# Staging slots, a shorter w2 ring, swapped pools and a re-ordered last norm in a float32 trunk layer

## The chip, the cores and the metric

One core of a Trainium2 chip. The metric is the device time of one execution in microseconds (us); the time before is the median of three executions. The engines are TensorE (PE), VectorE (DVE), ScalarE (ACT), GpSimd (POOL) and SyncE (SP, which here issues DMAs only). All instructions of one engine run in the order of the program.

## What is computed

One layer of a trunk on 2048 positions of width 1024, all in float32: a token mixer (left as it is here) and a feed-forward part.

```python
def reference(x, ...):
    h = x
    for l in range(DEPTH):                     # DEPTH = 1
        y = rmsnorm(h, pre_mix_g[l])
        ...
        h = h + rmsnorm(m, post_mix_g[l])
        f = rmsnorm(h, pre_ff_g[l]) @ w_ff1[l]           # 2048x1024 @ 1024x4096
        f = jnp.square(jax.nn.relu(f)) @ w_ff2[l]        # 2048x4096 @ 4096x1024
        h = h + rmsnorm(f, post_ff_g[l])
    return h
```

## The kernel before

**Stages.** In the trace the mixer runs to about 783 us, the first product of the feed-forward part (FF1) from there to about 1430, the second (FF2) from 1431 to the end. A float32 product is made of three matmuls in a split form: each operand is a high part (a cast by ACT) and a low part (a difference by VectorE); `mm3` (L142) does low x high, high x high, high x low, and `split_lo` (L139) makes the low part. Both products of the feed-forward part use one level of Winograd's scheme, so that a block product takes seven (p1 to p7) and not eight, on operands that are sums of quarters.

**FF1.** `seq` lists 224 ticks: 32 steps (two passes p over halves of the positions, 16 steps q over w1), each with seven products; a tick is one product, 12 matmuls of 128x512. Work of the other engines is planned to ticks by hand: `plan(tick, fn, ...)` appends to a tick's list and `do(tick)` runs the list after the tick's matmuls and its evacuation. The right operand `ht` (the transposed h, 28 tiles, each high and low) belongs to a pass and is replaced at the change of pass, ticks 104 to 114. `ht_in(1, n)` reads tile n into a staging slot (hr) on SP, and `ht_split` splits it; the slots are the four of the tag `four`. Two pools lie next to each other here: `fr` with the ring `w2s` (three tiles of 128x1024) and `wq` with the split w1 tiles `wh` and `wl`.

**W2 in FF1's shadow.** W2 is cut into 16 quarters q; `read_w2` reads one into `w2s`, `sum_w2` makes the sums t1 to t4 on VectorE, and `split_w2` casts (ACT), subtracts (VectorE) and stores both parts (th and tl) to memory, `t_d`, by the queue of POOL. The parts lie in the same four `four` slots. `when(j)` gives the tick of a quarter's j-th job: the ticks from 36 on, 11 a quarter, with the ticks of the change of pass left out (`away`).

**End of FF1.** The result of a step lies in ux and uy (128x1024 each) and is written to `f_d` on SP, a tick after its last operation (`keep_f`).

**FF2.** 16 chunks m = (p, c): two passes p, eight slices c of the inner dimension. A chunk has seven products in the order p1, p6, p5, p7, p4, p3, p2, each for four row tiles r: 28 slots of 6 matmuls. The right operand tt (1 MB a product, three buffers, read on SP two products ahead) comes from `t_d`. The left operand of the next chunk is made from f (512 KB reads on SP) by the jobs of `PREP`, planned to slots by `plan2`: a sum is VectorE's, a split is a cast on ACT (sh) and a difference on VectorE (sl). `SHIFT` delays the jobs of some chunks. After a slot's matmuls `evac` takes its bank: in a pass's first chunk ACT copies it into an accumulator (`acc`, 28 tiles), later VectorE adds it. In the last chunk of a pass the rows are finished: ACT sums squares (jq), `root` makes 1/rms with VectorE and a POOL power, `scale` multiplies by it and by post_ff_g, `give` adds the residual (hr) and writes the row to `out`. Rows of a pass come in two sets of four, from p7 and p4 (rows 4 to 7, later 12 to 15) and from p3 and p2 (rows 0 to 3, later 8 to 11).

**Order around the end of a pass.** In a slot the planned jobs come first, then the list `soon` (roots of the slot before), then `evac`. After pass 0 a list `tail` holds 16 jobs, one taken per slot of chunk 8: for each row a `scale`, and `pair_up` with the other `scale`, two residual additions on POOL and two writes by POOL's queue. After pass 1 POOL multiplies each half by post_ff_g (`weigh`, 12 times), and VectorE finishes with one operation a half (`finish_row`).

## Time and profile before

| | us |
|---|---|
| median of three executions | 2112.43 (2110.93 to 2113.45) |
| the profiled execution | 2111.22 |
| its span in the trace | 2109.5 |
| PE busy | 2020.6 (96%) |
| DVE busy | 1428.3 (68%) |
| ACT busy | 996.9 (47%) |
| POOL busy | 279.6 (13%) |

The profile is of one execution, and its span is 1.7 us shorter than that execution's time. Shares of the whole span are averages over the stages; TensorE's two clock levels are 2.4 GHz (granted clock 1.00) and 1.2 GHz (0.50). Rows of the trace stand below, in groups, where the prediction reads them.

### The profile page before, as it was taken

What the parts mean: (1) busy time and instruction counts of PE and PEld (TensorE: products, weight loads), DVE (VectorE), ACT (ScalarE), POOL (GpSimd) and SP (SyncE); (2) the same over time, 40 slices, a digit from 0 to 9 for tenths busy, and PEclk for the clock granted to TensorE, in tenths of its full rate; (3) what the DMA queues carried; (4) which work ended last, traced back from release to release, by engine and by line L of the source; (5) the groups of instructions that cost most, each with busy time, mean ns of one, the idle gap of its engine ahead of it and who ended that gap; (6) DMA issues with size and microseconds to landing.
All of it is one profiled execution on the core that took longest, in us unless ns stands there. A gap on an engine that the chain in (4) does not pass through costs nothing.

```text
span 2109.5 us, 27460 instructions
## 1 busy us (share of the span) xinstructions
PE 2020.6 (96%) x9504; PEld 1660.1 (79%) x9504; DVE 1428.3 (68%) x2463; ACT 996.9 (47%) x1966; POOL 279.6 (13%) x427
## 2 busy tenths in 40 slices
PE   8999999999899998999998999998999998999994
PEld 6888878888788877888876888886888886788883
DVE  3484467357646776666667666665788888988884
ACT  5463465356345556566667666666222225322112
POOL 0020011002101100022211222220000004200004
PEclk9999999999999999999999999999999999999997
DMA  6444244425843457768777877778667666776655
GB/s 211 123 116 131 80 135 144 157 76 176 251 154 98 158 189 219 254 250 273 258 254 256 281 260 250 269 265 316 236 229 269 239 223 241 284 268 241 259 188 191
DMA packets 164716, 446.86 MB, mean 212 GB/s; under 512 B 23376, under 2 KB 48480, under 8 KB 150240
## 3 DMA queue, kind: packets, MB, share of 16 engines
q1 hardware_dynamic: 139040, 359.09, 50.8%
q0 software_dynamic: 25536, 86.00, 11.2%
q8 instruction: 75, 1.23, 0.2%
q14 instruction: 65, 0.53, 0.1%
HBM read 319.19 MB, written 125.83 MB: 211 GB/s over the span
## 4 chain that ended last, share of the span: by engine, by line
PE 76%; DVE 8%; DMA 7%; ACT 4%; issue 3%; POOL 2%; SPq 0%; POOLq 0%; ACTq 0%; DVEq 0%
PE pf_A L143 5%; PE pf_A L144 5%; PE pf_A L145 5%; PE po_A L144 5%; PE po_A L143 5%; PE po_A L145 5%; PE pp_o L143 3%; PE pp_o L145 2%; PE pp_o L144 2%; PE pf_C L143 2%; PE pf_C L145 2%; PE pf_C L144 2%; PE po_C L144 2%; PE po_C L143 2%; PE po_C L145 2%
## 5 line engine op out<-in xcount | busy, mean ns | idle before, releaser
L493 DVE TENSOR_TENSOR acc_p<-acc_p,po_A 128x512 f32<-128x512 f32 x224 | 153.6, 686 | 21.8 <-PE po_A L145 6.7
L953 ACT CAST sh_s<-r 128x512 fp32r<-128x512 f32 x96 | 56.7, 619 | 186.0 <-PE po_A L145 118.7
L140 DVE TENSOR_TENSOR wl_s<-s,wh_s 128x512 fp32r<-128x512 f32 x96 | 66.2, 689 | 71.9 <-ACT wh_s L691 71.8
L143 PE MATMUL pf_A<-hl_t,wh_s 128*128 128x512 f32 x256 | 102.3, 400 | 12.6 <-ACT uy L878 9.1
L143 PE MATMUL po_A<-tt,sh_a 128*128 128x512 f32 x256 | 102.0, 398 | 8.3 <-DMA tt<-t_d_b 6.0
L143 PE MATMUL po_A<-tt,sh_s 128*128 128x512 f32 x256 | 100.8, 394 | 6.9 <-DVE acc_p L493 3.1
L143 PE MATMUL pp_o<-wl_o,abh 128*128 128x512 f32 x256 | 103.3, 404 | 2.1 <-DVE h L450 1.9
L953 ACT CAST sh_a<-f 128x512 fp32r<-128x512 f32 x96 | 57.5, 620 | 99.5 <-PE po_C L144 37.7
L144 PE MATMUL po_A<-tt,sh_a 128*128 128x512 f32 x256 | 102.1, 399 | 0.0
L145 PE MATMUL po_A<-tt,sl_a 128*128 128x512 f32 x256 | 101.8, 398 | 0.0
L144 PE MATMUL pf_A<-hh_t,wh_s 128*128 128x512 f32 x256 | 101.7, 397 | 0.0
L145 PE MATMUL pf_A<-hh_t,wl_s 128*128 128x512 f32 x256 | 101.4, 396 | 0.0
L144 PE MATMUL po_A<-tt,sh_s 128*128 128x512 f32 x256 | 101.2, 395 | 0.0
L145 PE MATMUL po_A<-tt,sl_s 128*128 128x512 f32 x256 | 100.9, 394 | 0.0
L218 DVE SCALAR_TENSOR_TENSOR wl_o<-ws_o,outg,wh_o 128x512 fp32r<-128x512 f32 x64 | 47.9, 749 | 78.0 <-ACT wh_o L217 78.0
L144 PE MATMUL po_C<-tt,sh_s 128*128 128x512 f32 x256 | 100.5, 393 | 0.0
L145 PE MATMUL pp_o<-wh_o,abl 128*128 128x512 f32 x256 | 100.4, 392 | 0.0
L144 PE MATMUL pp_o<-wh_o,abh 128*128 128x512 f32 x256 | 100.3, 392 | 0.0
L143 PE MATMUL po_C<-tt,sh_s 128*128 128x512 f32 x256 | 99.9, 390 | 0.4 <-DMA tt<-t_d_t 0.4
L145 PE MATMUL po_C<-tt,sl_s 128*128 128x512 f32 x256 | 100.2, 391 | 0.0
L140 DVE TENSOR_TENSOR wl_a<-w1s,wh_a 128x512 fp32r<-128x512 f32 x96 | 65.9, 687 | 45.3 <-ACT wh_a L691 45.2
L217 ACT ACTIVATE wh_o<-ws_o,outg 128x512 fp32r<-128x512 f32 x64 | 46.3, 723 | 100.7 <-PE pp_o L145 56.2
(292 smaller groups left out, 6069.0 us busy)
## 6 DMA issues: line engine op xcount, KB each, us to landing
tt<-t_d_t SPq DMA_DIRECT2D x64, 1024.0 KB, 4.8
tt<-t_d_b SPq DMA_DIRECT2D x48, 1024.0 KB, 4.8
w1s<-in_w SPq DMA_DIRECT2D x64, 512.0 KB, 4.9
f<-f_d SPq DMA_DIRECT2D x64, 512.0 KB, 7.1
ws_o<-in_w_out SPq DMA_DIRECT2D x64, 256.0 KB, 2.5
w2s<-in_w POOLq DMA_DIRECT2D x32, 512.0 KB, 5.7
t_d_t<-th_t POOLq DMA_DIRECT2D x64, 256.0 KB, 4.7
t_d_t<-tl_t POOLq DMA_DIRECT2D x64, 256.0 KB, 4.7
```

Of the source, the lines that this page charges most:

```text
L140: v.tensor_tensor(out_lo, src, hi.bitcast(F32), ALU.subtract)
L143: pe.matmul(ps, ahi, blo, start=start, stop=False, **kw)
L144: pe.matmul(ps, ahi, bhi, start=False, stop=False, **kw)
L145: pe.matmul(ps, alo, bhi, start=False, stop=stop, **kw)
L217: a.activation(hi, st, AF.Copy, scale=gain)
L218: v.scalar_tensor_tensor(lo, st, gain, hi.bitcast(F32), ALU.mult, ALU.subtract)
L493: eng.tensor_tensor(out_, x_, y_, ALU.add)
L953: a.copy(hi, src)
```

## The change

1. **Staging at FF1's change of pass.** The 28 reads of the second pass use 12 slots and not four: the four `four` slots, two `hts` slots and six halves of the `w2s` ring. Their reads are planned further ahead, and the splits stand at the front of their tick's list.
2. **w2 ring.** A quarter takes 10 ticks and not 11, from tick 44 and not 36.
3. **Pools.** `ga` (accumulators) and `gt` (tt) change places on the right side, so that tt lies over `fr`, and the accumulators over `wq`. The first chunk's a11 splits lie in the ring `h` of another pool.
4. **Splits of the left operand** become two jobs: `high_f` (ACT's cast) before `evac` and `low_f` (VectorE's difference) after it. Roots come after `evac`, a slot after their last square. `SHIFT` covers one chunk more.
5. **End of pass 0.** `tail` holds four jobs a row (32), one a slot and two in each fourth; the residual additions are VectorE's, the writes stay on POOL's queue.
6. **End of pass 1.** `weigh` and `finish_row` are gone; a row's root comes a slot after its last square and its scalings and additions two slots after. The additions of rows 12 to 15 are POOL's, those of rows 8 to 11 VectorE's, the writes go by SP.

```diff
     def ht_in(p, n):
-        staged[p, n] = slot(f"hr{p}_{n}", tag="four") if p else stage(f"hr{p}_{n}")
-        read_ht(p, n, staged[p, n])
+        if p == 0:
+            st = stage(f"hr{p}_{n}")
+        elif n % 12 < 4:
+            st = slot(f"hr{p}_{n}", tag="four")
+        elif n % 12 < 6:
+            st = wp.tile([P, 512], F32, name=f"hr{p}_{n}", tag="hts", bufs=2)
+        else:
+            if n % 2 == 0:
+                staged["two"] = fr.tile([P, D], F32, name=f"hr{p}_{n}", tag="w2s", bufs=3)
+            st = staged["two"][:, n % 2 * H:(n % 2 + 1) * H]
+        staged[p, n] = st
+        read_ht(p, n, st)
...
     for n in range(28):
-        plan(at[NQ - 1, FIRST[n // 4]] + 1, ht_in, 1, n)
-        plan(at[NQ - 1, FIRST[n // 4]] + 2, ht_split, 1, n)
+
+        plan(at[NQ - 1, FIRST[n // 4 - 3]] + 2 if n >= 12 else at[NQ - 1, "p1"] + 1 + n // 8, ht_in, 1, n)
+    for n in range(28):
+        todo.setdefault(at[NQ - 1, FIRST[n // 4]] + 2, []).insert(n % 4, (ht_split, (1, n)))
...
-    free = [t for t in range(36, len(seq)) if t not in away]
+    free = [t for t in range(44, len(seq)) if t not in away]
     for q in range(NQ):
         def when(j):
-            return free[11 * q + j]
+            return free[10 * q + j]
...
-            (5, sum_w2, "t3"), (6, split_w2, "t1"), (7, split_w2, "t3"), (8, sum_w2, "t4"), (9, split_w2, "t4"),
-            (10, split_w2, "b22"),
+            (4, split_w2, "t2"), (5, split_w2, "t1"), (6, sum_w2, "t4"), (7, split_w2, "t3"), (8, split_w2, "t4"),
+            (9, split_w2, "b22"),
...
+    ga = ctx.enter_context(tc.tile_pool(name="ga", bufs=1, side="right", reuse_waits="tile"))
     gt = ctx.enter_context(tc.tile_pool(name="gt", bufs=1, side="right", reuse_waits="tile"))
-    ga = ctx.enter_context(tc.tile_pool(name="ga", bufs=1, side="right", reuse_waits="tile"))
...
-    SHIFT = {NC: 12, NC + 1: 9, NC + 2: 6, NC + 3: 3}
+    SHIFT = {NC: 12, NC + 1: 12, NC + 2: 9, NC + 3: 6, NC + 4: 3}
...
-    def give(i, hf, eng):
+    def give(i, hf, eng, queue):
         plus(eng, res[i][hf], res[i][hf], halves[i, hf])
-        queue = pool if eng is pool else dma
         queue.dma_start(out[i * P:(i + 1) * P, hf * 512:(hf + 1) * 512], res[i][hf])
...
+        if hf:
+            return
+        soon.setdefault(slot_ + 1, []).append((root, row_))
         if p < NP - 1:
-            if done:
-                tail.extend(((scale, row_, 0), (pair_up, row_)))
-            return
-        if n != "p2":
-            weigh(row_, hf)
-        if n == "p4":
-            soon.extend(((finish_row, row_, 0), (finish_row, row_, 1)))
-        elif n == "p2":
-            soon.extend(((finish_row, row_, 1), (scale, row_, 0), (give, row_, 0, v)))
+            tail.extend(((scale, row_, 1), (give, row_, 1, v, pool), (scale, row_, 0), (give, row_, 0, v, pool)))
+        else:
+            eng = pool if row_ == j else v
+            soon.setdefault(slot_ + 2, []).extend((
+                (scale, row_, 1), (give, row_, 1, eng, dma), (scale, row_, 0), (give, row_, 0, eng, dma)))
...
+                for fn, args in todo2.pop((slot_, 0), ()):
+                    fn(*args)
+                evac(m, n, r, banks[chain, r])
                 for fn, args in todo2.pop(slot_, ()):
                     fn(*args)
-                for fn, *args in soon:
+                for fn, *args in soon.pop(slot_, ()):
                     fn(*args)
-                soon.clear()
-                evac(m, n, r, banks[chain, r])
-                if tail and c < NC - 1:
...
+                for _ in range((2 if slot_ % 4 == 3 else 1) if c < NC - 1 else 0):
+                    if tail:
+                        fn, *args = tail.pop(0)
+                        fn(*args)
+
+                        nth = 8 - len(tail) // 4
+                        if len(tail) % 4 == 0 and 2 <= nth < 6:
+                            read_h(nth - 2)
```

**SP at FF1's change of pass**, from the fourth read of the new right operand (hr1_3) on; w1s are halves of w1 for a coming step, f_d writes are results of step 14. Before:

```order
L526 DMA hr1_3_10911<-ht_d2_95 128x512
L668 DMA w1s17_0_10930<-in_w1 128x1024
L850 DMA f_d0_14_111<-ux14_10699 128x1024
L850 DMA f_d0_14_111<-uy14_10700 128x1024
L526 DMA hr1_4_10991<-ht_d2_95 128x512
L526 DMA hr1_5_10993<-ht_d2_95 128x512
L526 DMA hr1_6_10995<-ht_d2_95 128x512
L526 DMA hr1_7_10997<-ht_d2_95 128x512
L668 DMA w1s17_1_11018<-in_w1 128x1024
L524 DMA hr1_8_11036<-b_d1_0_133 128x512
L524 DMA hr1_9_11038<-b_d1_1_134 128x512
L524 DMA hr1_10_11040<-b_d1_2_135 128x512
```

After, from the same place in the queue:

```order
L526 DMA hr1_3_10899<-ht_d2_95 128x512
L526 DMA hr1_4_10901<-ht_d2_95 128x512
L526 DMA hr1_5_10903<-ht_d2_95 128x512
L526 DMA hr1_6_10905<-ht_d2_95 128x512 x2
L668 DMA w1s17_0_10941<-in_w1 128x1024
L524 DMA hr1_8_10943<-b_d1_0_133 128x512
L524 DMA hr1_8_10943<-b_d1_1_134 128x512
L524 DMA hr1_10_10946<-b_d1_2_135 128x512
L524 DMA hr1_10_10946<-b_d1_3_136 128x512
L524 DMA hr1_12_10949<-b_d1_0_133 128x512
L524 DMA hr1_13_10951<-b_d1_1_134 128x512
L524 DMA hr1_14_10953<-b_d1_2_135 128x512
```

The reads of tiles 4 to 15 moved ahead of the f_d writes, most of them ahead of the second w1 half.

**VectorE in chunk 7**, at product p4 of pass 0's last chunk: acc0_p4 are evacuations of four row tiles, sl8 splits for chunk 8, r2 one of its sums, ssf and rs_f the roots of rows 4 and 5. Before:

```order
L493 TENSOR_TENSOR acc0_p4_0_14288<-acc0_p4_0_14288,po7_A_0_16204 128x512
L496 TENSOR_TENSOR r2_8_1_16393<-r1_8_1_16366,f8_0_1_16123 128x512
L1021 TENSOR_TENSOR ssf4_16325<-ssf4_16325 128x1
L152 TENSOR_SCALAR rs_f4_16396<-ssf4_16325 128x1
L493 TENSOR_TENSOR acc0_p4_1_14300<-acc0_p4_1_14300,po7_A_1_16213 128x512
L140 TENSOR_TENSOR sl8_0_s2_16409<-r2_8_0_16382,sh8_0_s2_16408 128x512
L1021 TENSOR_TENSOR ssf5_16341<-ssf5_16341 128x1
L152 TENSOR_SCALAR rs_f5_16413<-ssf5_16341 128x1
L493 TENSOR_TENSOR acc0_p4_2_14314<-acc0_p4_2_14314,po7_A_2_16222 128x512
L140 TENSOR_TENSOR sl8_1_s2_16426<-r2_8_1_16393,sh8_1_s2_16425 128x512
```

After:

```order
L493 TENSOR_TENSOR acc0_p4_1_14291<-acc0_p4_1_14291,po7_A_1_16205 128x512
L496 TENSOR_TENSOR r2_8_1_16388<-r1_8_1_16362,f8_0_1_16116 128x512
L1053 TENSOR_TENSOR ssf4_16316<-ssf4_16316 128x1
L152 TENSOR_SCALAR rs_f4_16391<-ssf4_16316 128x1
L493 TENSOR_TENSOR acc0_p4_2_14303<-acc0_p4_2_14303,po7_A_2_16214 128x512
L140 TENSOR_TENSOR sl8_0_s2_16401<-r2_8_0_16377,sh8_0_s2_16400 128x512
L1053 TENSOR_TENSOR ssf5_16332<-ssf5_16332 128x1
L152 TENSOR_SCALAR rs_f5_16408<-ssf5_16332 128x1
L493 TENSOR_TENSOR acc0_p4_3_14317<-acc0_p4_3_14317,po7_A_3_16223 128x512
L140 TENSOR_TENSOR sl8_1_s2_16418<-r2_8_1_16388,sh8_1_s2_16417 128x512
```

An evacuation that stood behind a split and a root stands ahead of them now, one row tile further.

**VectorE at the end**, products p4 and p3 of the last chunk (acc1), with the roots and norms of rows 12 to 14. Before:

```order
L493 TENSOR_TENSOR acc1_p4_1_16836<-acc1_p4_1_16836,po15_A_1_18765 128x512
L1021 TENSOR_TENSOR ssf13_18886<-ssf13_18886 128x1
L152 TENSOR_SCALAR rs_f13_18963<-ssf13_18886 128x1
L1040 SCALAR_TENSOR_TENSOR hr13_18890<-acc1_p4_1_16836,rs_f13_18963,hr13_18890 128x512
L1040 SCALAR_TENSOR_TENSOR hr13_18890<-acc1_p7_1_16777,rs_f13_18963,hr13_18890 128x512
L493 TENSOR_TENSOR acc1_p4_2_16848<-acc1_p4_2_16848,po15_A_2_18774 128x512
L1021 TENSOR_TENSOR ssf14_18899<-ssf14_18899 128x1
L152 TENSOR_SCALAR rs_f14_18985<-ssf14_18899 128x1
L1040 SCALAR_TENSOR_TENSOR hr14_18903<-acc1_p4_2_16848,rs_f14_18985,hr14_18903 128x512
L1040 SCALAR_TENSOR_TENSOR hr14_18903<-acc1_p7_2_16792,rs_f14_18985,hr14_18903 128x512
L493 TENSOR_TENSOR acc1_p4_3_16857<-acc1_p4_3_16857,po15_A_3_18783 128x512
```

After:

```order
L493 TENSOR_TENSOR acc1_p4_2_16812<-acc1_p4_2_16812,po15_A_2_18766 128x512
L1059 SCALAR_TENSOR_TENSOR acc1_p7_0_16731<-acc1_p7_0_16731,rs_f12_18931,pfg_13990 128x512
L1059 SCALAR_TENSOR_TENSOR acc1_p4_0_16786<-acc1_p4_0_16786,rs_f12_18931,pfg_13990 128x512
L1053 TENSOR_TENSOR ssf13_18877<-ssf13_18877 128x1
L152 TENSOR_SCALAR rs_f13_18954<-ssf13_18877 128x1
L493 TENSOR_TENSOR acc1_p4_3_16825<-acc1_p4_3_16825,po15_A_3_18775 128x512
L1059 SCALAR_TENSOR_TENSOR acc1_p7_1_16747<-acc1_p7_1_16747,rs_f13_18954,pfg_13990 128x512
L1059 SCALAR_TENSOR_TENSOR acc1_p4_1_16797<-acc1_p4_1_16797,rs_f13_18954,pfg_13990 128x512
L1053 TENSOR_TENSOR ssf14_18889<-ssf14_18889 128x1
L152 TENSOR_SCALAR rs_f14_18977<-ssf14_18889 128x1
L493 TENSOR_TENSOR acc1_p3_0_16842<-acc1_p3_0_16842,po15_C_0_18820 128x512
```

The two scalings of a row moved behind the evacuation of a later row tile and now write the accumulator; the residual additions to hr12 to hr15, which L1040 contained, are POOL's.

## Rows read from the trace of the kernel before

**Rows 1.** length; busy us (count) of PE, PEld, DVE, ACT, POOL; clock; DMA; GB/s

```profile
1085.00:1132.00 47.00, 37.10 (x150) 28.48 (x149) 32.27 (x50) 32.07 (x57) 1.08 (x2) 0.93 0.77 244
...
1430.00:1453.00 23.00, 15.42 (x54) 11.52 (x53) 15.22 (x25) 14.17 (x28) 1.10 (x2) 0.85 0.97 363
1453.00:1738.00 285.00, 285.00 (x1246) 233.83 (x1246) 228.35 (x353) 71.68 (x127) 0.46 (x1) 1.00 0.67 244
1738.00:1815.00 77.00, 66.07 (x255) 51.23 (x254) 65.73 (x84) 37.42 (x77) 38.51 (x44) 0.91 0.68 256
...
2060.00:2110.00 50.00, 18.51 (x71) 14.36 (x69) 24.20 (x49) 9.07 (x26) 18.74 (x22) 0.70 0.51 187
```

**Rows 2.** the same view, of the half-clock stretch in chunk 7

```profile
1746.00:1752.80 6.80, 5.99 (x14) 4.52 (x15) 5.43 (x10) 3.40 (x9) 0.55 (x1) 0.50 0.27 111
```

**Rows 3.** waits of PE, 1085 to 1132: us in total, times, longest

```profile
PE pf_A L143 <- ACT uy L878: 9.1, 2, 8.1
```

**Rows 4.** timeline of SP, change of pass: start, length, instruction

```profile
1084.78 5.72 SPq L526 DMA_DIRECT2D hr<-ht_d  x4
```

**Rows 5.** timeline of ACT there, in brackets the idle time before

```profile
1121.02 0.62 ACT L537 CAST hh_t<-hr 128x512 fp32r<-128x512 f32 x1 [0.66 <-DMA hr<-b_d]
```

**Rows 6.** busy by stretch again, inside chunk 8, for DMA

```profile
1763.00:1802.00 39.00, 35.83 (x146) 28.00 (x146) 38.97 (x36) 19.77 (x38) 30.44 (x32) 0.96 0.89 340
1775.00:1780.00 5.00, 5.00 (x22) 4.09 (x23) 5.00 (x5) 1.76 (x3) 4.49 (x5) 1.00 1.02 425
```

**Rows 7.** waits of PE, 1430 to 1453

```profile
PE po_A L143 <- DMA tt<-t_d_b: 6.0, 1, 6.0
```

**Rows 8.** timeline of SP at the start of FF2

```profile
1430.64 0.32 SPq L961 DMA_DIRECT2D tt<-t_d_b  x1
```

**Rows 9.** chain that ended last, chunk 7: start, length, what

```profile
1743.26 0.61 DVE acc_p L493
...
1746.16 0.61 DVE acc_p L493
```

**Rows 10.** waits of PE, 1738 to 1815

```profile
PE po_A L143 <- DMA tt<-t_d_t: 3.2, 2, 2.3
PE po_A L143 <- DVE acc_p L493: 3.1, 1, 3.1
PE po_B L143 <- DVE acc_p L493: 2.9, 1, 2.9
```

**Rows 11.** groups of DVE, 1763 to 1810: busy us, mean ns, idle before

```profile
L140 DVE TENSOR_TENSOR sl_s<-r,sh_s 128x512 fp32r<-128x512 f32 x6 | 10.8, 1828 | 0.0
```

**Rows 12.** groups of DVE, 1453 to 1738

```profile
L140 DVE TENSOR_TENSOR sl_s<-r,sh_s 128x512 fp32r<-128x512 f32 x41 | 28.1, 685 | 5.4 <-ACT sh_s L953 5.4
```

**Rows 13.** DMA issues, 1738 to 1815: KB each, median us to landing

```profile
out<-hr POOLq DMA_DIRECT2D x16, 256.0 KB, 6.3
hr<-h_d POOLq DMA_DIRECT2D x4, 512.0 KB, 7.2
```

**Rows 14.** waits of PE from 2060

```profile
PE po_B L143 <- DVE acc_p L493: 12.0, 1, 12.0
```

**Rows 15.** chain that ended last, from 2060

```profile
2075.79 1.41 DVE hr L1040 x2
...
2079.96 0.52 POOL rs_f L153
2080.50 1.41 DVE hr L1040 x2
...
2104.18 0.69 DVE hr L493
```

**Rows 16.** groups of POOL, 2055 to 2110

```profile
L1037 POOL TENSOR_TENSOR acc_p<-acc_p,pfg 128x512 f32<-128x512 f32 x12 | 15.3, 1293 | 260.5 <-ACT jq L1017 260.4
```

**Rows 17.** DMA issues of FF1, 783 to 1430

```profile
t_d_t<-th_t POOLq DMA_DIRECT2D x64, 256.0 KB, 4.7
```

**Rows 18.** waits of ACT, 783 to 1430

```profile
ACT th_b L814 <- DMA t_d_t<-th_t: 2.3, 1, 2.3
```

More of the change, by code (lines that the diff above doesn't have):

```diff
@@ L833, in trunk @@
         if q + 1 < NQ:
-            plan(when(2), read_w2, q + 1, 0)
-            plan(when(8), read_w2, q + 1, 1)
+            if when(10) - when(9) > 1:
+                plan(when(10) - 2, read_w2, q + 1, 0)
+                plan(when(10) - 2, read_w2, q + 1, 1)
+            else:
+                plan(when(2), read_w2, q + 1, 0)
+                plan(when(8), read_w2, q + 1, 1)
     banks, us = {}, {}
@@ L947, in sum_f, with high_f, low_f @@
             minus(v, part[name], part["a12"], part["s2"])
-    def split_f(m, name, kk):
+    def high_f(m, name, kk):
         src = fsrc[m, kk][name]
-        hi = g.tile([P, H], F32R, name=f"sh{m}_{kk}_{name}", tag="s", bufs=NSP)
-        lo = g.tile([P, H], F32R, name=f"sl{m}_{kk}_{name}", tag="s", bufs=NSP)
+        if (m, name) == (0, "a11"):
+            st = wp.tile([P, RP], F32R, name=f"s{m}_{kk}_{name}", tag="h", bufs=4)
+            hi, lo = st[:, 0:H], st[:, H:RP]
+        else:
+            hi = g.tile([P, H], F32R, name=f"sh{m}_{kk}_{name}", tag="s", bufs=NSP)
+            lo = g.tile([P, H], F32R, name=f"sl{m}_{kk}_{name}", tag="s", bufs=NSP)
         a.copy(hi, src)
-        split_lo(lo, src, hi)
         left[m, name, kk] = hi, lo
+    def low_f(m, name, kk):
+        hi, lo = left[m, name, kk]
+        split_lo(lo, fsrc[m, kk][name], hi)
     def read_t(j):
@@ L981, in trunk @@
         o = 28 * (m - 1) + SHIFT.get(m, 0)
-        for n, fn, name, kk in PREP:
-            plan2(o + n, fn, m, name, kk)
+        for n, what, name, kk in PREP:
+            if what == "sum":
+                plan2(o + n, sum_f, m, name, kk)
+            else:
+                plan2((o + n, 0), high_f, m, name, kk)
+                plan2(o + n, low_f, m, name, kk)
         if m + 1 < NCH:
@@ L992, in trunk @@
     read_t(1)
-    for n, fn, name, kk in PREP:
-        fn(0, name, kk)
+    for n, what, name, kk in PREP:
+        if what == "sum":
+            sum_f(0, name, kk)
+        else:
+            high_f(0, name, kk)
+            low_f(0, name, kk)
     for n in range(2):
@@ L1000, in trunk @@
     halves, res = {}, {}
-    tail, soon = [], []
+    tail, soon = [], {}
     def read_h(i, early=False):
@@ L1027, in scale @@
         v.scalar_tensor_tensor(x_, x_, halves[i, "r"], pfg[:, cs], ALU.mult, ALU.mult)
-    def give(i, hf, eng):
+    def give(i, hf, eng, queue):
         plus(eng, res[i][hf], res[i][hf], halves[i, hf])
-        queue = pool if eng is pool else dma
         queue.dma_start(out[i * P:(i + 1) * P, hf * 512:(hf + 1) * 512], res[i][hf])
-    def weigh(i, hf):
-        cs = slice(hf * 512, (hf + 1) * 512)
-        pool.tensor_tensor(halves[i, hf], halves[i, hf], pfg[:, cs], ALU.mult)
-    def finish_row(i, hf):
-        v.scalar_tensor_tensor(res[i][hf], halves[i, hf], halves[i, "r"], res[i][hf], ALU.mult, ALU.add)
-        dma.dma_start(out[i * P:(i + 1) * P, hf * 512:(hf + 1) * 512], res[i][hf])
-    def pair_up(i):
-        scale(i, 1)
-        give(i, 0, pool)
-        give(i, 1, pool)
     def evac(m, n, r, ps_):
@@ L1116, in trunk @@
                 slot_ += 1
-    for fn, *args in soon:
-        fn(*args)
+    for t in sorted(soon):
+        for fn, *args in soon[t]:
+            fn(*args)
 def _constants():
```

18 lines of the change are left out of this document (2 added, 16 removed), and 6 rows, old and new, of the table PREP.

## The prediction

> **What bounds the kernel now.** I read the busy shares first (TensorE leads by far), then a table by stretch, then in each poor stretch the waits of TensorE, the chain that ended last, and the groups of the engine that TensorE waited for. From 1453 to 1738 us TensorE is busy all of 285.00 us at granted clock 1.00 (2.4 GHz): 1246 matmuls, 0.2287 us each [rows 1]. That is the yardstick: a stretch loses its length less 0.2287 us times its matmuls, which counts gaps and half-speed matmuls together. Change of pass in FF1 (1085 to 1132): 47 - 150 x 0.2287 = 12.7. FF1 to FF2 (1430 to 1453): 23 - 54 x 0.2287 = 10.7. Change of pass in FF2 (1738 to 1815): 77 - 255 x 0.2287 = 18.7. End (2060 on): 50 - 71 x 0.2287 = 33.8, with all that comes after the last matmul [rows 1]. Some 76 us in all; the change works at exactly these four places. Behind a gap the clock stands at 0.50 (1.2 GHz): 14 matmuls in 5.99 us, 0.43 each, so a gap brings a second bill of 0.2 us a matmul, 2.8 us here [rows 2].
>
> A tick of FF1 is 12 matmuls, 2.74 us; a slot of FF2 is 6, 1.372; a chunk of 28 slots is 38.4. Up to 783 us the instructions are the same and in the same order: nothing there.
>
> **1. Change of pass in FF1.** TensorE waits 9.1 us, 8.1 of it at once, for ACT to evacuate a bank [rows 3]. ACT isn't overloaded: it works in order and stands before splits of the new right operand, whose reads are late; the last of these splits that waited for its read, that of the 20th, began at 1121.02 [rows 5]. The reads are late because SP holds them, each until one of four staging slots has been split. With 12 slots up to 12 reads are under way. By the order listing SP must bring the first 20 reads (5.2 MB), two w1 halves and two f writes (2.1 MB), 7.3 MB in all, from about 1090.5, when the first four had been issued (1084.78 + 5.72 [rows 4]; they wait for the stores of the last w2 quarter, and still do). At the 340 GB/s of a full stretch [rows 6] that ends at 1112; at the 244 of this stretch [rows 1], at 1120.5. For the gap of 8.1 us to go, the 20th must land 8.1 us before 1121.0, at 1113. The 340 leaves nothing of the gap, the 244 nearly all of it. Since the 244 contains the slot waits that go away, I take 300: landed at 1115, 2 us of gap and a little clock, and the other 1 us of waiting, which I make half a microsecond longer, because the splits now stand at the front of their tick, ahead of the w1 split that TensorE wants. Left 4.5 of 12.7: **gain 8**, bounds 1 and 11. Queued behind a late read are, on SP, the w1 reads, and on ACT the evacuations, as before.
>
> **2. The w2 ring, 10 ticks a quarter for 11.** The same operations, started 8 ticks later and done 8 ticks earlier, so that its stores and reads are out of the way at the end of FF1. They lie beside TensorE, which is the slower one per tick: **0**. What is new is a shorter distance between two uses of a slot, in rival C.
>
> **3. FF1 to FF2.** TensorE waits 6.0 us for the first tt [rows 7]. Its read is issued at 1430.64 [rows 8], in SP's order behind a write of f_d that waits for the square of the last ux; it stands there still. The swap of pools changes what tt waits for in memory (the end of the last p7 instead of the last matmuls, a product earlier) but not that queue. The evacuation order and the empty POOL queue give about 1 us of start and landing: **gain 1**, bounds 0 and 9 (most of gap and clock, if the queue is not what holds it). The a11 splits moved to another ring are ready before tt either way, at cost nothing; without that cover they would cost the 2 x 0.61 us of two of them.
>
> **4. Change of pass in FF2.** Three things. First, while the last products of chunk 7 are evacuated, each slot takes a round of VectorE (evacuation), ACT (square, then cast) and VectorE (split), and the next evacuation starts behind it: 1743.26, then 1746.16 [rows 9], 2.9 us for 1.372 us of TensorE. In the order of VectorE, split and root now stand behind the evacuation of their slot, so that the evacuation doesn't wait for a cast that waits for the square of the one before; without the round VectorE has two operations of 0.61 and two tiny ones, about 1.5 us a slot, near TensorE's pace. That takes away the wait of 2.9 us [rows 10] and most of the half-clock bill of 2.8 [rows 2]; 1 may stay: 4.7. Second, in chunk 8 VectorE works while POOL adds residuals, and its operations stretch: splits of 1828 ns on the mean [rows 11] instead of 685 [rows 12]. The adds move to VectorE: 16 x 0.61 = 9.8 us more. With 16 scalings of 0.70 [rows 15] (11.2) and 22 splits and sums of the next chunk of 0.61 (13.4) it has 34.4 us of work for chunk 8's 38.4 us: covered, with 4 us to spare. This takes off the other wait for VectorE, 3.1 us [rows 10], and its clock bill: 5. Third, the stalls on tt, 3.2 us [rows 10], and all that is left of the 18.7, some 5.8 (clock and small gaps): the SP order of those reads does not change, but the 32 pieces of tail work are spread over 26 slots, not 16, with their writes. I leave 2 to 3 us there, and take 6.3. Together 4.7 + 5 + 6.3: **gain 16**, bounds 6 (rival A) and 18.
>
> This adds a wait: VectorE's add wants the residual row, which VectorE did not before. Behind it stand evacuations, for which TensorE waits. A row's four pieces take 3.2 slots, 4.4 us; the read of row 0 is issued when the write of row 4 has landed and is used three rows later, some 13 us, against a write and a read at 6.3 and 7.2 us [rows 13]: just in time, 0 by these medians.
>
> The 1828 against 685 ns is the ground for the second step. The Trainium skill (SBUF — State Buffer, "SBUF: two separate sides") says the pair of ports shared by VectorE and GpSimd is an exclusive lock, held for a whole instruction, also by a VectorE operation with two SBUF inputs against a GpSimd operation that reads SBUF. By that rule the stretch goes entirely when POOL has no adds, as I take it; the rows agree, and without the rule one could leave half of it to another cause, such as the transfers, and take 2.5 for that 5.
>
> **5. The end.** TensorE waits 12.0 us for VectorE in one piece [rows 14]. VectorE stands before two scalings that wait for POOL, which has 12 multiplications of 1293 ns [rows 16] ahead of its roots: from scaling to scaling 2075.79 to 2080.50, 4.7 us a row [rows 15]. After: POOL has per row a root of 0.52, waits for a scaling of 0.70, and does two adds like its 1293 ns, 3.8 us, to 4.65 if VectorE's second scaling and the first add hold each other up. But two evacuations of the next product now come between the rows, so the p2 matmuls start some 11 us before the end of that wait, and then go at VectorE's pace. Rows 8 to 11 then cost VectorE 2 x 0.70 + 2 x 0.61 and 0.33 for the root, 3 us a row, with POOL's root hidden behind the row ahead; before, each took 4.6 with the root on the path. Following the order by hand, the last add comes at 2095.6 to 2098.5 where it ended at 2104.87 [rows 15], with the same writing out behind: a gain of 6.4 to 9.3, **I take 8**, bounds 3 (every POOL add held to 4.65 and the first row late) and 10.
>
> **Sum.** 8 + 0 + 1 + 16 + 8 = 33. The profiled execution took 2111.2 (span 2109.5 and 1.7 around it), the median is 2112.4: 2112.4 - 33 = 2079.
>
> **Rivals.**
> A. Chunk 8 is bound by its transfers. Its 38.4 us must carry 7 tt of 1.05 MB, 4 f of 0.52, 16 writes of 0.26 and 4 residual reads of 0.52: 15.7 MB, 409 GB/s. For it: from 1763 to 1802 the mean was 340 GB/s. Against it: 5 us of that moved 425 [rows 6]. At 340 the transfers take 46.2 us, 7.8 more, with a clock bill of 2: gain 6 instead of 16, 2089. The Trainium skill (DMA: Bandwidth & Descriptors, "Where 436 GB/s comes from") gives a core some 358 GB/s from HBM; by it the chunk would take 43.9 us, an estimate, and this rival would hold in part. The row of 425 GB/s is above that, so I don't take it as a wall.
> B. The change does not do what it says at FF1's change of pass: bytes, not slots, hold the reads, at 244 GB/s again. Gain 1 there: 2086.
> C. **Slower.** Of the slots in which a w2 quarter is split, one pair is now used again after 2 ticks (5.5 us) and not 3. A store lands 4.7 us after its issue [rows 17]; with split and issue about 6.5 us after the cast, so ACT waits 1 us once a quarter, which TensorE's other bank hides. Before, the longest such wait was 2.3 us [rows 18]; if every quarter met a store as late, it would be 2.3 + 2.74, less one tick that is hidden, so 2.3 us for each of 16 quarters: 37 us, 2116. It decides from 2.1 us a quarter. Against it: that wait is 2.3 us in one place, not in all.
> D. tt comes early at FF1 to FF2 and no clock is lost there: 8 more, 2071.
>
> **Chances.** Forecast 0.58 (2072 to 2085), A 0.22, B 0.08, C 0.04, D 0.08. A and B together give 2096; the best bounds of the other terms (-3, -2, -2) with D give 2064; so the range is 2064 to 2097. About 0.2% (4 us) is what can be told from no change. Faster: all but C and 0.02 of luckless sums, 0.94; same 0.02; slower 0.04.
>
> **What would show it.** Change of pass in FF1: the reads issued within a few us of each other and no gap of 8 us. FF1 to FF2: the same wait for tt, about 5 us. FF2: splits near 685 ns everywhere, no round of 2.9 us in chunk 7, VectorE nearly without idle time but ahead of TensorE; if A holds, waits for tt or for hr with the DMA share near 1. End: rows 8 to 11 about 3 us apart. Wrong if ACT shows waits for t_d stores in each quarter, or if the adds on VectorE push evacuations back by more than a slot.

## The result and the profile after

The changed kernel takes 2088.6 us (median; 2087.7 to 2089.3) against 2112.9 of the kernel before in the same job: a ratio of 0.9879 with a 95% interval of 0.9856 to 0.9902, 24.3 us faster. The forecast was 2079 and 33 us, the range 2064 to 2097: sign and range hold, a quarter of the gain is missing. The time lies outside the 2072 to 2085 that had most of the chance, at rival A's 2089, and A's mechanism did not come (below): so part of this is luck. The profiled execution took 2087.7, with a span of 2085.9.

The table by stretch, of the changed kernel (length; busy us and count of PE, PEld, DVE, ACT, POOL; granted clock; DMA share; GB/s):

```profile
1085.00:1132.00 47.00, 41.38 (x171) 32.73 (x170) 37.00 (x60) 35.83 (x67) 3.86 (x8) 0.96 0.86 297
1132.00:1425.00 293.00, 291.86 (x1262) 235.79 (x1261) 200.37 (x321) 191.62 (x341) 83.87 (x155) 1.00 0.76 264
1425.00:1456.00 31.00, 20.63 (x74) 15.34 (x73) 17.93 (x29) 15.98 (x31) 2.18 (x4) 0.89 0.86 339
...
1735.00:1812.00 77.00, 73.31 (x320) 59.55 (x319) 65.39 (x118) 38.70 (x80) 17.91 (x32) 1.00 0.88 338
1812.00:2050.00 238.00, 238.00 (x1041) 195.30 (x1040) 204.73 (x316) 52.53 (x96) 0.97 (x2) 1.00 0.65 240
2050.00:2086.00 36.00, 13.83 (x46) 9.65 (x44) 25.89 (x46) 6.17 (x18) 15.15 (x15) 0.72 0.43 158
```

By the yardstick of [rows 1] (length less 0.2287 us a matmul) TensorE's losses are:

| place | before | after | gain | forecast |
|---|---|---|---|---|
| change of pass in FF1 | 12.7 | 47 - 171 x 0.2287 = 7.9 | 4.8 | 8 |
| FF1 to FF2 | 10.7 | 31 - 74 x 0.2287 = 14.1 | -3.4 | 1 |
| change of pass in FF2 | 18.7 | 77 - 320 x 0.2287 = 3.8 | 14.9 | 16 |
| from there to the end of the span | 294.5 - 1143 x 0.2287 = 33.1 (from 1815) | 273.9 - 1087 x 0.2287 = 25.3 | 7.8 | 8 |

The rest, FF1's second pass, lost 0.7 more. Together 23.4; the spans differ by 23.6.

What TensorE waits for at the four places, in the changed kernel, one view for each (us in total, times, longest); they answer to [rows 3], [rows 7], [rows 10] and [rows 14]. At the change of pass in FF1:

```profile
PE pf_A L143 <- ACT uy L894: 5.6, 2, 3.5
```

From FF1 to FF2, the same view:

```profile
PE po_A L143 <- DMA tt<-t_d_b: 4.9, 1, 4.9
PE po_C L143 <- DMA tt<-t_d_t: 3.0, 1, 3.0
PE po_A L143 <- ACT acc_p L1070: 2.4, 2, 1.6
```

At the change of pass in FF2, the same view:

```profile
PE po_A L143 <- DMA tt<-t_d_t: 1.9, 1, 1.9
PE po_A L143 <- DVE acc_p L493: 1.8, 1, 1.8
```

And at the end:

```profile
PE po_B L143 <- DVE acc_p L493: 5.5, 3, 2.7
```

The long waits are gone (8.1 and 12.0 us in one piece). At the start of FF2 the first one fell from 6.0 to 4.9 as forecast, but two others grew, on the third tt and on ACT's copies. In the kernel before they were, in the same view (1430 to 1453):

```profile
PE po_A L143 <- ACT acc_p L1053: 1.2, 1, 1.2
PE po_C L143 <- DMA tt<-t_d_t: 0.4, 1, 0.4
```

### The profile page after: what moved, and what is told of

Read it like the earlier page. It is cut to its first block, busy times and chain, and to the rows that moved or that the text cites. A ratio compares the mean times of both kernels' runs of the same rounds, so it can differ in the third digit from the quotient of the medians.

```text
span 2085.9 us, 27424 instructions
## 1 busy us (share of the span) xinstructions
PE 2014.2 (97%) x9504; PEld 1656.1 (79%) x9504; DVE 1424.2 (68%) x2483; ACT 995.7 (48%) x1966; POOL 253.4 (12%) x407
## 4 chain that ended last, share of the span: by engine, by line
PE 76%; DMA 9%; DVE 5%; issue 4%; ACT 3%; POOL 2%; SPq 0%; POOLq 0%; DVEq 0%; ACTq 0%
PE po_A L143 5%; PE po_A L144 5%; PE po_A L145 5%; PE pf_A L143 5%; PE pf_A L144 4%; PE pf_A L145 4%; PE pp_o L143 3%; PE po_C L143 3%; PE pp_o L145 2%; PE po_C L144 2%; PE po_C L145 2%; PE pp_o L144 2%; PE pf_C L145 2%; PE pf_C L144 2%; PE pf_C L143 2%
## 5 line engine op out<-in xcount | busy, mean ns | idle before, releaser
L143 PE MATMUL po_A<-tt,sh_a 128*128 128x512 f32 x248 | 97.4, 393 | 0.0
L144 PE MATMUL po_A<-tt,sh_a 128*128 128x512 f32 x248 | 97.1, 391 | 0.0
L145 PE MATMUL po_A<-tt,sl_a 128*128 128x512 f32 x248 | 96.6, 390 | 0.0
```

Source lines behind the costliest of these rows:

```text
L143: pe.matmul(ps, ahi, blo, start=start, stop=False, **kw)
L144: pe.matmul(ps, ahi, bhi, start=False, stop=False, **kw)
L145: pe.matmul(ps, alo, bhi, start=False, stop=stop, **kw)
```

## The experiments

Each kernel is the changed one with the edit shown. The executions of the kernel before spread from 2110 to 2126 us over the chips used, more than most edits are worth. So the verdicts rest on places: TensorE's loss there in the trace, here summed from the gaps (start to start above 0.2287 us, half-clock matmuls included).

| kernel | pass, FF1 | FF1 to FF2 | pass, FF2 | end, PE only | time, ratio to before |
|---|---|---|---|---|---|
| before | 12.6 | 10.8 | 18.5 | 14.5 | |
| changed | 7.7 | 14.3 | 4.1 | 8.6 | 2088.6, 0.9879 |
| four slots | **20.9** | 13.3 | 5.8 | 8.6 | 2101.4, 0.9926 |
| splits at the back | **8.0** | 13.7 | 4.9 | 7.8 | 2088.9, 0.9873 |
| half the reads | **8.3** | 12.1 | 2.7 | 8.6 | 2087.7 (one run) |
| half the splits | **3.9** | 15.5 | 4.2 | 8.5 | 2087.3 (one run) |
| w2 ring of 11 | 8.1 | **16.6** | 6.1 | 8.6 | 2092.6, 0.9890 |
| a11 in g | 9.0 | **10.6** | 7.3 | 6.3 | 2090.5, 0.9871 |
| pools as before | 8.5 | **11.1** | 5.5 | 6.5 | 2089.4, 0.9866 |
| residual reads on SP | 8.2 | **8.3** | 4.4 | 6.3 | 2085.5, 0.9834 |
| additions on POOL | 8.8 | 12.8 | **7.0** | 8.3 | 2093.7, 0.9896 |
| evacuation last | 6.8 | 14.0 | **14.3** | 8.3 | 2096.9, 0.9906 |
| four parts | 8.2 | **8.7** | **1.9** | **2.6** | 2069.7, 0.9793 |
| and later jobs | 8.0 | **9.8** | 1.6 | 2.6 | 2072.8, 0.9800 |

One execution of each kernel is traced, and a place that an edit leaves alone varies too: the change of pass in FF1 from 6.8 to 9.0 us over the kernels of the table, FF1 to FF2 from 12.1 to 15.5, the change of pass in FF2 from 2.7 to 7.3. The end with what follows the last matmul varies less, from 25.4 to 25.9. A difference inside these spreads shows nothing.

### The change of pass in FF1: slots, bytes or work

Four slots, reads planned as before:

```diff
-        elif n % 12 < 4:
+        elif True:
             st = slot(f"hr{p}_{n}", tag="four")
...
-        plan(at[NQ - 1, FIRST[n // 4 - 3]] + 2 if n >= 12 else at[NQ - 1, "p1"] + 1 + n // 8, ht_in, 1, n)
+        plan(at[NQ - 1, FIRST[n // 4]] + 1, ht_in, 1, n)
```

> The changed kernel with four staging slots for all 28 reads and the reads planned as before; the splits stay at the front of their tick. Theory of the prediction (slots hold the reads): the loss of TensorE at the change of pass in FF1 goes from 7.7 back to 12 to 13 us, time 2093 to 2094. Rival (the bytes or the work of ACT and VectorE set it, the slots do little): 8 to 9 us, time 2088 to 2090.

The waits of TensorE in that stretch of this kernel:

```profile
PE pf_A L143 <- ACT uy L894: 11.0, 2, 6.1
PE pf_C L143 <- ACT wh_s L691: 1.5, 1, 1.5
```

The loss is 20.9, worse than the kernel before: with the splits at the front of the tick the slots are worth 13 us here, and a loss of 12 to 13, as the theory had it, was too low. TensorE waits for the evacuations (11.0) and now for w1 splits too. That splits at the front of a tick with reads this late make ACT stand longer is the likely reason; it was not tried apart.

Splits at the back of the list:

```diff
-        todo.setdefault(at[NQ - 1, FIRST[n // 4]] + 2, []).insert(n % 4, (ht_split, (1, n)))
+        plan(at[NQ - 1, FIRST[n // 4]] + 2, ht_split, 1, n)
```

> The changed kernel, 12 staging slots kept, but each split of the new right operand is appended to its tick's list, as before the change, behind the w1 split and the sums of that tick. Theory (work in order): what is left at the change of pass in FF1, 7.7 us, is no longer the reads but the casts and differences themselves, 28 x 0.52 us on ACT and 28 x 0.61 on VectorE, which stand ahead of the evacuations and w1 splits that TensorE wants; behind them the 7.7 become 4 to 6. Theory (bytes): the reads still set it, 7.7 to 8.5 stay. Third: the splits now come too late for TensorE, and it waits for hh and hl instead, above 9.

8.0, and two waits for ACT as before: with 12 slots the place in the list decides nothing. This fits the theory of bytes, so the next two take one cause away each. Half the reads:

```diff
     def ht_in(p, n):
+        if p == 1 and n >= 8 and n % 2:
+            return
...
     def ht_split(p, n):
-        split_ht(p, n, staged.pop((p, n)))
+        if p == 1 and n >= 8 and n % 2:
+            split_ht(p, n, staged.pop((p, n - 1)))
...
```

> The changed kernel with bytes taken away at the change of pass in FF1: of the tiles 8 to 27 of the new right operand only every second one is read, and its neighbour is split from the same staged tile (all casts and differences stay; the left-out reads make the output another one). 10 reads of 0.26 MB less, 2.6 of some 11 MB. Theory (bytes): the second gap, 3.7 us at 1123, closes and the loss of 7.7 falls to 3 or 4. Theory (the order and the work of ACT and VectorE): it stays at 7 to 8.

Half the splits:

```diff
     def ht_split(p, n):
+        if p == 1 and n >= 8 and n % 2:
+            staged.pop((p, n))
+            (key, k), (key0, k0) = PAIRS[n], PAIRS[n - 1]
+            ht[p, key, k] = ht[p, key0, k0]
+            return
         split_ht(p, n, staged.pop((p, n)))
```

> The changed kernel with work taken away at the change of pass in FF1: of the tiles 8 to 27 every second one is read but not split, and its neighbour's parts are used in its place (all reads stay; the left-out splits make the output another one). 10 casts of 0.52 us on ACT and 10 differences of 0.61 on VectorE less. Theory (work): 5 to 6 us less on either engine, the second gap closes and the loss falls from 7.7 to 3 or 4 (the first gap of 2.3 us, ahead of tile 8, stays). Theory (bytes): 7 to 8 us stay.

TensorE's waits in that stretch, with half the reads:

```profile
PE pf_A L143 <- ACT uy L901: 4.8, 2, 2.5
```

The same view, with half the splits:

```profile
PE pf_A L143 <- ACT uy L899: 2.1, 1, 2.1
```

Without 2.6 MB the loss is 8.3, inside the spread; without 10 casts and 10 differences it is 3.9, one wait of two left. So the longer of the two waits is the work of ACT and VectorE (the run doesn't part the two engines), not the reads. The trace of the changed kernel shows it as well: the 20th read lands at 1113.7 us, and from the fifth cast on no cast waits for its read. ACT's timeline ahead of the copy that ends the longer wait:

```profile
1117.65 0.63 ACT L856 ACTIVATE uy<-uy 128x512 f32<-128x512 f32 x1 [1.76 <-DVE uy L493]
...
1118.86 2.16 ACT L537 CAST hh_t<-hr 128x512 fp32r<-128x512 f32 x4
...
1122.64 0.57 ACT L894 COPY uy<-pf_A 128x512 f32<-128x512 f32 x1
```

ACT waits for VectorE, and then the copy stands behind four casts and other work. The table by stretch, of these 30 us (columns as above):

```profile
1097.00:1127.00 30.00, 24.38 (x98) 18.97 (x98) 25.75 (x43) 26.92 (x51) 1.10 (x2) 0.94 0.97 341
```

VectorE is busy for 25.8 of them and ACT for 26.9. The shorter wait, 2.1 us at 1100, stays in both runs; the first four casts, just ahead of it, wait 5.0 us for their reads, and that was not tested.

### The w2 ring

```diff
-    free = [t for t in range(44, len(seq)) if t not in away]
+    free = [t for t in range(38, len(seq)) if t not in away]
...
-            return free[10 * q + j]
+            return free[11 * q + j]
...
```

(with the jobs of a quarter in their order of before).

> The changed kernel with 11 ticks a w2 quarter from tick 38 (so that a quarter still ends ahead of the change of pass), the jobs of a quarter as before the change. Theory (the shorter ring is nearly free): ACT's waits for t_d stores in FF1 fall from 9.7 us in all to under 4, but TensorE gains at most 0.8 us by that, the loss of 1.7 in FF1's second pass becoming 0.9; the stores run to the end of FF1 and meet the first tt: 1 to 3 us more from 1425 to 1470. Time 2088 to 2091. Rival C of the prediction (the shorter ring costs): 3 us or more are gained in FF1.

ACT's waits for stores in FF1, in the changed kernel:

```profile
ACT th_b L826 <- DMA t_d_b<-th_b: 5.5, 3, 2.6
ACT th_b L826 <- DMA t_d_t<-th_t: 3.6, 5, 0.9
```

TensorE's waits at the start of FF2, with 11 ticks:

```profile
PE po_A L143 <- DMA tt<-t_d_b: 12.1, 1, 12.1
```

With 11 ticks ACT never waits for a store. But the first tt, which needs the last stores, now comes 12.1 us late, against 4.8 to 5.6 in the kernels that leave this place alone, and the loss is 16.6, above their spread. In FF1's second pass the run loses 0.9 and the changed kernel 1.7; that is not the ring's price, since eight kernels of the table with 10 ticks a quarter lose 0.9 there too, though in one of them (four parts) ACT waits 16.5 us for stores. So the shorter ring costs TensorE nothing that shows, and brings a little at the start of FF2. Rival C is out.

### The start of FF2

POOL's residual reads of rows 4 to 7 in the changed kernel (timeline of POOL; in brackets the idle time before and what ended it):

```profile
1428.92 0.55 POOL L1042 DMA_DIRECT2D hr<-h_d  x1 [28.67 <-ACT sh_s L974]
1434.11 0.55 POOL L1042 DMA_DIRECT2D hr<-h_d  x1 [4.64 <-ACT sh_s L974]
1438.14 0.54 POOL L1042 DMA_DIRECT2D hr<-h_d  x1 [3.48 <-PE po_A L145]
1438.84 0.54 POOL L1042 DMA_DIRECT2D hr<-h_d  x1 [0.16 <-issue]
```

The program has them in chunk 7, 290 us later. But POOL has nothing to do in between, so each goes out as soon as the ring `h` has a free tile, here among the first reads of tt and f. In the kernel before two of them went out at 1419. Three kernels change this. Reads on SP:

```diff
-            pool.dma_start(st, h_d[i])
+            (dma if i % 8 >= 4 else pool).dma_start(st, h_d[i])
```

> The changed kernel, but the residual reads of rows 4 to 7 and 12 to 15 are issued on SP and not on POOL. Theory (floating reads): POOL has nothing ahead of these reads, so they go out as soon as their ring has a free tile, at 1428.9 to 1438.8 us in the changed kernel, among the first tt and f reads of FF2, and at 1793 to 1797, at the end of chunk 8. In SP's order they go out in chunk 7, where the DMA engines have room. Then the loss of TensorE from 1425 to 1470 falls from 14.3 to 9 to 11 us (2.1 MB at 400 GB/s are 5 us, of which some is hidden), the 2.1 us of waiting for tt at 1807 go, and the time is 2082 to 2085 for 2088.6. Rival (the stretch is long because of the swapped pools and the bytes of tt and f alone): 14 us stay, and the time is within 1 us of 2088.6.

The timeline of SP in this kernel:

```profile
1721.89 2.08 SPq L1042 DMA_DIRECT2D hr<-h_d  x4
```

And TensorE's waits at the start of FF2:

```profile
PE po_A L143 <- DMA tt<-t_d_b: 5.2, 1, 5.2
PE po_C L143 <- DMA tt<-t_d_t: 1.0, 1, 1.0
```

The reads are now in chunk 7; the loss falls from 14.3 to 8.3, well below the spread, the waits for ACT go, that for the third tt falls from 3.0 to 1.0. The wait for tt in chunk 9 went as well, while that for VectorE there grew from 1.8 to 2.5. The time, 2085.5, is just above what was expected, and the profiled execution (2087.2) is only 0.5 us faster than that of the changed kernel. The table by stretch shows where its gain went; first the changed kernel, then this one:

```profile
1830.00:2030.00 200.00, 200.00 (x875) 164.09 (x875) 171.93 (x265) 40.90 (x70) 0.00 (x0) 1.00 0.67 243
...
1830.00:2030.00 200.00, 200.00 (x859) 162.01 (x858) 168.90 (x261) 40.27 (x69) 0.00 (x0) 1.00 0.65 237
```

From about 1795 us to 2060 matmuls start 0.2333 us apart here and not 0.2289, without a gap and at a granted clock of 1.00: some 5 us. The trace doesn't show why. The traced execution of the kernel "evacuation last" has the same from 1808 us on, and no other one has it in FF2. The a11 splits back in g:

```diff
-        if (m, name) == (0, "a11"):
+        if False:
```

> The changed kernel, but the first chunk's a11 splits lie in the pool g, as before the change. Theory (floating reads): those splits took the ring h, and so held back the residual reads that went out at 1419 in the kernel before; with the ring free two of the four go out before FF1 ends, and the loss from 1425 to 1470 falls from 14.3 by 2 to 3 us, to 11.5 or 12. Rival (pool swap): 14.3 stays. A third possibility: a11 in g waits for memory of FF1 and the first matmul comes later, then the loss is above 15.

TensorE's first wait in this kernel:

```profile
PE po_A L143 <- ACT sh_s L974: 5.1, 1, 5.1
```

Two reads leave at 1413.9 and 1416.4, as the theory had it, and the loss is 10.6, about that of before. The first wait is as long as ever, but it ends with a cast of ACT and not with tt, so something of the third possibility is in it too. The time, 2090.5 of two executions, is no better. And the pools in the order of before:

```diff
-    ga = ctx.enter_context(tc.tile_pool(name="ga", bufs=1, side="right", reuse_waits="tile"))
     gt = ctx.enter_context(tc.tile_pool(name="gt", bufs=1, side="right", reuse_waits="tile"))
+    ga = ctx.enter_context(tc.tile_pool(name="ga", bufs=1, side="right", reuse_waits="tile"))
```

> The changed kernel with the pools of tt and accumulators in the order of before. Theory (SP's order of the first tt behind the f_d write sets its start, the swap hardly matters): the first wait for tt grows by at most 1.5 us (5.05 to 6.5), the rest stays, time 2088 to 2090. Rival (the swap costs the 3 us at the start of FF2): the loss from 1425 to 1470 falls from 14.3 to 11. Rival (the swap saves the queue): the first wait grows by 3 us or more.

The loss is 11.1, near what the rival had, with a first wait of 5.2, which is inside the 4.8 to 5.6 of the others. In its trace two of the four reads go out at 1441, 3 us later than in the changed kernel; but with the additions on POOL, where this place is left alone, they go out at 1440 and the loss is 12.8. So the swap gained nothing that shows on the first wait and may have lost 1 to 3 us behind it; whether it did, and whether by the reads alone, stays open. With the reads gone and the swap kept (8.3) there is no loss against the kernel before.

### The change of pass in FF2

```diff
-            ... (give, row_, 1, v, pool), (scale, row_, 0), (give, row_, 0, v, pool)))
+            ... (give, row_, 1, pool, pool), (scale, row_, 0), (give, row_, 0, pool, pool)))
```

> The changed kernel with the residual additions of pass 0 on POOL again (the scalings, the spreading over the slots and the queue of the writes as changed). Theory of the prediction (VectorE's operations stretch beside POOL's additions): the splits sl_s in chunk 8 go from some 690 ns to over 1500, VectorE is full, and the loss of TensorE around the change of pass in FF2 goes from 4.1 to 8 or 11 us; time 2093 to 2096. Rival (the spreading did it, or the transfers): 3 to 6 us, time 2087 to 2091; below 4.1 if VectorE's waits for residual rows, which this takes away, cost more than the stretch.

VectorE's groups from 1752 to 1800 in the changed kernel (busy us, mean ns | idle before and what ended it):

```profile
L493 DVE TENSOR_TENSOR hr<-hr,acc_p 128x512 f32<-128x512 f32 x16 | 11.0, 690 | 6.5 <-issue 3.7 <-DMA hr<-h_d 1.0 <-DVE acc_p L1059 0.8
...
L140 DVE TENSOR_TENSOR sl_s<-r,sh_s 128x512 fp32r<-128x512 f32 x7 | 4.8, 684 | 0.0
```

The same view, with the additions on POOL:

```profile
L140 DVE TENSOR_TENSOR sl_s<-r,sh_s 128x512 fp32r<-128x512 f32 x6 | 6.4, 1075 | 0.0
```

And TensorE's wait for VectorE around the change of pass in this kernel:

```profile
PE po_A L143 <- DVE acc_p L493: 3.6, 1, 3.6
```

The split takes 684 ns while POOL has no additions and 1075 beside them: the stretch is shown. Its price is not: TensorE's wait for VectorE is 3.6 us, above the 0 to 2.4 of the kernels that leave this place alone, but the loss of 7.0 for 4.1 lies inside the spread of this place. This run also takes away VectorE's waits for residual rows, which work the other way. Next, evacuation last:

```diff
-                evac(m, n, r, banks[chain, r])
                 for fn, args in todo2.pop(slot_, ()):
                     fn(*args)
                 for fn, *args in soon.pop(slot_, ()):
                     fn(*args)
+                evac(m, n, r, banks[chain, r])
```

> The changed kernel, with the evacuation of a slot again behind the difference of its split and behind the roots. Theory of the prediction (a round of VectorE, ACT and VectorE per slot): evacuations 2.9 us apart at product p4 of chunk 7, TensorE waits 3 us there with a clock bill of 2 to 3: loss around the change of pass 9 to 10 us for 4.1, time 2093 to 2095. Rival (the round came of the roots alone or is hidden by the banks): 4 to 5 us, time 2088 to 2090. At the end of the kernel nothing is prepared any more, so only the roots move: within 1.5 us there.

The chain that ended last in this kernel, in chunk 7 (start, length, what):

```profile
1735.93 0.60 DVE acc_p L493
...
1738.84 0.60 DVE acc_p L493
```

And TensorE's waits around the change of pass:

```profile
PE po_B L143 <- DVE acc_p L493: 3.4, 2, 2.9
PE po_A L143 <- DVE acc_p L493: 2.5, 1, 2.5
```

The round of 2.9 us is back (the next two evacuations follow at 1741.74 and 1744.64), and with it a loss of 14.3, 10.2 more than in the changed kernel and 7.0 more than the highest of those that leave this place alone. That is more than the 4.7 that I gave it: the delay goes on into chunks 8 and 9. The traced execution is the slowest of four (2101.5; the median is 2096.9), and some 5 us of it are the slower matmuls told of above, which lie behind this place.

### A version from these runs

Four parts: the reads on SP; the last step's writes after the first reads of FF2; rows 0 to 3 read in chunk 7 into tiles of the split ring; at the end no addition on POOL, the weight multiplied in ahead of the root.

```diff
+        if s == NST - 1:
+            return
         if n == "p4":
             plan(i + 1, keep_f, s, 0)
...
+                if slot_ in (5, 6):
+                    keep_f(NST - 1, slot_ - 5)
...
-                        if len(tail) % 4 == 0 and 2 <= nth < 6:
-                            read_h(nth - 2)
...
-                if c == NC - 1 and n7 == 4 and p == NP - 1:
+                if c == NC - 1 and n7 == 4:
...
+            soon.setdefault(slot_ + 1, []).insert(0, (root, row_))
+            soon.setdefault(slot_ + 2, []).extend(((finish, row_, 1), (finish, row_, 0)))
```

> A version from what the runs so far show; each part works in a place of its own. (1) The residual reads of rows 4 to 7 and 12 to 15 on SP, as in the run on that. (2) The writes of the last step's results follow the first reads of tt and f in SP's order instead of preceding them. If the write ahead of it holds the first tt (the prediction's reason, rival D), the wait of 5 us for it goes to 1.5 or less, and the loss from 1425 to 1470 from 8.3 to 3 or 4; if the change of the memory's owner or bandwidth holds it, 4 to 5 us of that wait stay. (3) The residual rows 0 to 3 are read on SP in chunk 7 into tiles of the split ring, not by POOL when a written row's tile is free. If VectorE's waits for these rows make the gap in chunk 9, its 1.9 to 2.7 us go and the loss around the change of pass falls from 4.1 to under 2; if VectorE has no room, it stays. (4) At the end POOL only makes the roots; VectorE multiplies by the weight ahead of the root and finishes with one operation a half. If POOL's additions hold up VectorE there (scaling rows 4.3 us apart), the rows come 3 us apart and the end comes 5 to 7 us earlier; if VectorE's own work sets it, within 2. All: 2068 to 2074.

TensorE's waits in this version, at the start of FF2:

```profile
PE po_A L143 <- ACT acc_p L1079: 5.8, 1, 5.8
```

The same view, around the change of pass:

```profile
PE po_A L143 <- DMA tt<-t_d_t: 1.8, 1, 1.8
```

And at the end:

```profile
PE po_B L143 <- DVE acc_p L493: 2.0, 2, 1.2
```

2069.7 us, 0.9793 (0.9776 to 0.9809), the fastest median of all. (2) The first tt is read at 1420.5 and not 1426.1, and the wait for it is gone: the write ahead of it did hold it. But a wait of 5.8 us for ACT's copies stands in its place, and the loss is 8.7 for 8.3: missed. (3) The wait for VectorE in chunk 9 is gone and the loss is 1.9, below the spread; that the residual rows did it is likely, but with half the reads that wait is absent too. (4) The end, from the last evacuations on, is 8.8 us shorter (PE's loss 8.6 to 2.6, and 17.3 to 14.5 after the last matmul), more than expected; rows 12 to 15 come 2.5 to 2.9 us apart. Which of its three changes (no addition on POOL, the weight ahead of the root, one operation a half) did it was not tried apart. The last run delays the jobs that ACT stands before:

```diff
-    SHIFT = {NC: 12, NC + 1: 12, NC + 2: 9, NC + 3: 6, NC + 4: 3}
+    SHIFT = {1: 10, 2: 7, 3: 4, 4: 2, NC: 12, NC + 1: 12, NC + 2: 9, NC + 3: 6, NC + 4: 3}
```

> The version with all four parts, and the jobs that make the left operands of chunks 1 to 4 delayed by 10, 7, 4 and 2 slots. Theory: in that version TensorE's one wait of 6.0 us at the start of FF2 comes of ACT, which in its order stands before the cast of chunk 1's f, read from 1433.2 and landed at 1437.2 and 1439.6, with the copies of chunk 0's banks behind it; with the casts 10 slots later the copies come on time, and the loss from 1420 to 1465 falls from 8.7 to 2 to 4 us, time 2063 to 2066 for 2069.7. Rival (the transfers of this stretch, tt and f, are the bound): the wait moves to tt, 7 to 9 us stay, and the time is 2068 to 2071.

TensorE's waits at the start of FF2 in this kernel:

```profile
PE po_C L143 <- DMA tt<-t_d_t: 4.6, 1, 4.6
PE po_A L143 <- ACT acc_p L1079: 1.5, 1, 1.5
```

2072.8, 0.9800 (0.9782 to 0.9818), and a loss of 9.8 there: no gain, and as the rival had it most of the wait moved to tt. That read stands in SP's order behind the f reads of chunk 1, which go out at 1430.6; issuing it ahead of them was not tried.

## Why the prediction was right or wrong

**Change of pass in FF1, 8 forecast, 4.8 measured.** That slots hold the reads was right (20.9 with four), and rival B falls with it. The reads came even a little earlier than worked out (297 GB/s for 300; the 20th landed at 1113.7 for 1115). The failed step is "landed at 1115, 2 us of gap": I took the gap that is left from the landing of the reads and never added up the casts and differences. It measured 3.5 us, with the reads long there, and goes with half of the splits (a loss of 3.9) and not with half of the reads (8.3). The other wait, 1.5 in the forecast, measured 2.1.

**w2 ring, 0 forecast.** This was right. ACT's waits for stores are there (10 us in all) and hidden. The 0.7 that FF1's second pass lost comes of one wait of 0.6 us, at 1164, which eight kernels with the same ring do not have. What I costed at nothing on the other side, stores out of the way at the end of FF1, is worth a little (16.6 without it, at most 15.5 with it).

**FF1 to FF2, 1 forecast, -3.4 measured: wrong sign.** (With the spread of this place, -1.3 to -4.7.) The first wait fell as worked out, from 6.0 to between 4.8 and 5.6, and the reason given for what is left of it, the write ahead on SP, is shown by the version without it. The failed step is "the a11 splits moved to another ring ... at cost nothing": I asked when they are ready, not who else wants tiles of that ring. It is the residual reads, which float on POOL's queue: with them on SP the loss is 8.3, and with a11 back in g, 10.6. Rival D had the right cause and a wrong price: the first wait goes, and nearly nothing is gained, since the next transfer is as late.

**Change of pass in FF2, 16 forecast, 14.9 measured**, from terms that missed: the round was worth 7 to 12 (14.3 against 2.7 to 7.3 without it) and not 4.7, and the price of VectorE's stretch, 5 in the sum, is not clear of the spread. The third term of 6.3, tt and small gaps by spreading the tail, no run tested apart. That the sum came within 1.1 is luck. The added wait, costed at 0 by medians of 6.3 and 7.2 us, came: in this stretch the write takes 8.8 and the read 8.5. VectorE is idle 6.5 us ahead of its additions (row above); the view puts only 1.0 of it down to the reads, but by the trace's landing times the first four residual reads land at 1773.3, 1778.6, 1784.0 and 1789.3 us, each 0.1 us ahead of the addition that ends an idle time. The chain of the changed kernel has write, read and addition:

```profile
1768.55 11.29 DMA out<-hr
1780.38 6.89 DMA hr<-h_d
...
1789.35 0.69 DVE hr L493
```

TensorE's wait of 1.8 us for VectorE comes behind it; it is gone where these rows are read earlier (four parts). Rival A did not come, though its premise, full transfers, did. The table by stretch, of chunk 8 in the changed kernel:

```profile
1752.00:1791.00 39.00, 39.00 (x172) 32.01 (x171) 31.09 (x49) 20.66 (x38) 11.24 (x20) 1.00 0.99 376
```

The DMA engines are full at 376 GB/s for 39 us, and TensorE is busy all of it; the two waits of 1.9 and 1.8 us come behind, in chunk 9. The rate is above the some 358 GB/s that the Trainium skill (DMA: Bandwidth & Descriptors, "Where 436 GB/s comes from") gives as the limit of a core at HBM. Here one core runs alone, and the measurement decides.

**The end, 8 forecast, 7.8 measured.** Rows 12 to 15 came 4.3 us apart (forecast 3.8 to 4.65), as worked out. Rows 8 to 11 came 3.9 to 4.1 apart and not 3: the failed step is "with POOL's root hidden behind the row ahead", for VectorE waits 0.4 to 0.7 us a row for it. Those rows alone are some 2.8 us more than in the sum, which still came out, so as much was gained elsewhere in it. Where is not shown, and no run takes this part of the change back by itself: the total is in part luck. Timeline of VectorE:

```profile
2048.76 1.41 DVE L1059 SCALAR_TENSOR_TENSOR acc_p<-acc_p,rs_f,pfg 128x512 f32<-128x512 f32 x2
2050.09 1.26 DVE L1053 TENSOR_TENSOR ssf<-ssf 128x1 f32<-128x1 f32 x1
...
2053.12 1.42 DVE L1059 SCALAR_TENSOR_TENSOR acc_p<-acc_p,rs_f,pfg 128x512 f32<-128x512 f32 x2 [0.99 <-POOL rs_f L153]
...
2067.39 0.75 DVE L1059 SCALAR_TENSOR_TENSOR acc_p<-acc_p,rs_f,pfg 128x512 f32<-128x512 f32 x1
...
2071.53 0.75 DVE L1059 SCALAR_TENSOR_TENSOR acc_p<-acc_p,rs_f,pfg 128x512 f32<-128x512 f32 x1 [0.42 <-POOL rs_f L153]
```
